# Projections summed kind by kind, and the substitution's transfers issued from POOL, in a hybrid encoder step

## The chip, the cores and the metric

One Trainium2 chip, one of its NeuronCores. The metric is the device time of one execution in microseconds (us). Engines: PE (TensorE, the matmuls; PEld is its weight load), DVE (VectorE), ACT (ScalarE), POOL (GpSimd), SP (SyncE, which here only issues transfers). Each engine works through its own list of instructions in the order in which the program lists them, and stands still where an instruction waits for a semaphore.

## What is computed

One layer of a streaming encoder, for 1024 prompt tokens and 64 sample tokens of width 1024: a modulation from a conditioning vector, a norm, one input projection whose columns feed four mixers, an output projection, a gated residual, then a SwiGLU feed-forward part. Cut to what matters:

```python
h = modulate(rms_norm(x), mod[0:3]);  u = h @ w_in
y = concat(conformer_conv(u), gated_deltanet(u), multi_scale_pool(u), stick_breaking_attention(u))
x = x + gate1 * (y @ w_out)
h = modulate(rms_norm(x), mod[3:6])
x = x + gate2 * ((silu(h @ w_gate) * (h @ w_up)) @ w_down)

# inside gated_deltanet, per chunk of 64 tokens and head:
lmat = where(strict, (kb @ k.T) * decay, 0)
sol  = triangular_solve(lmat + eye(64), rhs, lower=True, unit_diagonal=True)
S    = S * g_last + k_upd.T @ (u - w @ S)          # a scan over the chunks
```

## The kernel before

**Tokens and tiles.** The tokens run in two halves: A with 512 prompt tokens, B with the other 512 and the 64 sample tokens (576, in two PSUM chunks of 288 columns). Activations lie feature by feature: 8 tiles of 128 features by the tokens of a half. A weight tile is 128x1024: the 8 contraction tiles of 128 output features. The feed-forward part has 22 tiles of 128 hidden features (gate and up), taken in pairs, and a pair goes through `down` with a contraction of 2 tiles.

**Precision.** Every projection is done in split fp32: the weight as whi (rounded) and wlo (rest), the activation as hi and lo, and the product as wh·xh + wh·xl + wl·xh, three matmuls for each contraction tile, all summed in one PSUM bank. `load_w` (L313 to L324) loads a raw weight tile (SP), rounds it to whi (ACT, L117) and subtracts to wlo (DVE, L123); there are two buffers of each. The tiles hi0 to hi7 and lo0 to lo7 of the normed activations have one buffer each. They are written tile by tile by the modulation (ACT, L114, and DVE, L126).

**gemm_fm** (L342) is the projection: for each chunk of columns it takes a bank, and runs over the contraction tiles with all three products for each. It is called for the input projection (`gemm_out`, `sb_qk`), the output projection (`out_proj`), and gate, up and down of the feed-forward part (`ffn`). In the first stages it has two PSUM banks; late in the program (`wide`) it takes the eight banks of `BANKS` in turn, the bank "o" of the attention's output among them.

**The delta-rule part.** `dn_group` works on a group of up to four chunks, four heads: g1 and g2 (half A), g3 and g4 (half B), g5 (the sample tokens). The inverse of the triangular 64x64 matrix starts with its 16x16 diagonal blocks, by forward substitution on POOL, since a row of a block must become a row in one partition. The steps, each waiting for the one before: DVE writes nl, the strict products (L754); SP stores it to DRAM (nld, L777, two issues); SP loads the diagonal blocks back as rows (fsn, L782, four issues of 16x16x16, 16 KB each in runs of 64 bytes); POOL copies (L785) and does 29 small operations (L786, L135); SP stores the result (xd, L793, four issues); SP loads X (L796, two issues); PE turns X (pw0, L798), and the two doubling levels of the inverse follow. The whole chain is called nl to pw0 below.

**The rest around it.** `sb_attn` is the stick-breaking attention; POOL issues its loads of k, q and v (L501 to L507, and L540 to L544 for the sample tokens). At its end for the sample tokens, `sb_finish` takes four slices from the bank psOs: ACT copies a slice to sbo, DVE subtracts, SP stores it to DRAM (mixB), and the next slice needs the same sbo, which has one buffer.

**What sets the order.** The program is written operation by operation; a scheduler, told of priorities, puts the instructions of all parts into one list per engine. A change of one part re-lays the lists of all engines. A transfer keeps the queue of the engine that issues it.

Of the kernel before, what the change touches and what calls it, by code (L numbers as in the profile page):

```python
# [59 lines left out]
def hybrid_encoder_kernel(ctx: ExitStack, tc: tile.TileContext, io):  # L60
    nc = tc.nc
# [75 lines left out]
    def mm(out, lhsT, rhs, start=True, stop=True):  # L137
        return nc.tensor.matmul(out, lhsT=lhsT, rhs=rhs, start=start, stop=stop)  # L138
# [198 lines left out]
    def gemm_bank(name="pg"):  # L337
        turn[0] += 1
        pool, tag = BANKS[turn[0] % 8] if wide[0] else BANKS[0]
        return pool.tile([P, 512], F32, tag=tag, name=name)  # L340

    def gemm_fm(h, src, xh, xl, order, w=None, o=0):  # L342
        nk = len(order)
        wh, wl = w or load_w(src, nk * 128)
        out = []
        for c0, n in h.chunks:
            ps = gemm_bank()
            for i, k in enumerate(order):
                a, b = wh[:, o + k * 128:o + (k + 1) * 128], wl[:, o + k * 128:o + (k + 1) * 128]
                mm(ps[:, 0:n], a, xh[k][:, c0:c0 + n], i == 0, False)  # L350
                mm(ps[:, 0:n], a, xl[k][:, c0:c0 + n], False, False)
                mm(ps[:, 0:n], b, xh[k][:, c0:c0 + n], False, i == nk - 1)
            out.append((ps, c0, n))
        return out

    KALL = list(range(KT))
# [332 lines left out]
    def dn_group(h, feats, gate, D, ch0, nch, tok0, mtok0, S):  # L689
        w = 2 * nch * 64  # L690
# [3 lines left out]
        def T4(tag, bufs=1):  # L694
            return dn.tile([P, 576], F32, tag=tag, name=tag)[:, 0:128 * NCH]
# [13 lines left out]
        def PS(name):  # L709
            return PD(name)  # L710
# [31 lines left out]
        for pair in range(2):  # L742
            o = pair * nch * 64
# [24 lines left out]
        X, Y, W = T4("X"), T4("Y"), T4("W")  # L768
# [5 lines left out]
        nx = 2 * nch  # L774
        ext, ins = nld[samp_g], xd[samp_g]
        for hp in range(2):
            nc.sync.dma_start(out=ext[:, :, hp].rearrange("b i x c j -> (b i) (x c j)"), in_=nl[64 * hp:64 * hp + 64, 0:w])  # L777
        N = dn.tile([64, 256], F32, tag="fsn", name="fsn")[0:8 * nx]
        T = dn.tile([64, 256], F32, tag="fst", name="fst")[0:8 * nx]
        tmp = dn.tile([64, 64], F32, tag="fsu", name="fsu")[0:8 * nx]  # L780
        for q in range(4):
            nc.sync.dma_start(out=N[2 * nx * q:2 * nx * (q + 1)].rearrange("p (i j) -> p i j", j=16),  # L782
                              in_=ext[q, :, :, :, q].rearrange("i h x j -> (h x) i j"))
        N3, T3 = N.rearrange("p (i j) -> p i j", j=16), T.rearrange("p (i j) -> p i j", j=16)
        nc.gpsimd.tensor_copy(out=T, in_=N)  # L785
# [1 line left out]
        for k in range(1, 15):  # L787
            n = 15 - k
# [1 line left out]
            ptt(u3, N3[:, k + 1:16, k:k + 1].to_broadcast([8 * nx, n, k]), T3[:, k:k + 1, 0:k].to_broadcast([8 * nx, n, k]), ALU.mult)  # L790
            ptt(T3[:, k + 1:16, 0:k], T3[:, k + 1:16, 0:k], u3, ALU.add)
        for q in range(4):
            nc.sync.dma_start(out=ins[q, :, :, :, q].rearrange("i h x j -> (h x) i j"),  # L793
                              in_=T[2 * nx * q:2 * nx * (q + 1)].rearrange("p (i j) -> p i j", j=16))
        for hp in range(2):
            nc.sync.dma_start(out=X[64 * hp:64 * hp + 64, 0:w], in_=ins[:, :, hp].rearrange("b i x c j -> (b i) (x c j)"))  # L796
        pw = PS("pw0")
        flip(pw, blk(X))  # L798
        copy_a(Y[:, 0:w], pw[:, 0:w])
# [21 lines left out]
        for c in range(nch):  # L821
            pv2 = PS("pvn")
            for pair in range(2):
                j = (pair * nch + c) * 64
# [9 lines left out]
            for pair in range(2):  # L834
                j = (pair * nch + c) * 64
# [15 lines left out]
        m = T4("kbe").rearrange("p (a c) -> p a c", a=2)  # L851
# [183 lines left out]
    def out_proj(h):  # L1035
        hi, lo = [None] * KT, [None] * KT
        order = [6, 7, 4, 5, 0, 1, 2, 3]
        with tc.high_priority():
            spare = mix_tiles() if h.samp else None
            for i, k in enumerate(order):  # L1040
                if h.samp:
                    t = dn.tile([P, 576], F32, tag=f"f{1 + i % 2}", name="mixt")
                    hi[k], lo[k] = spare[2 * i], spare[2 * i + 1]
                else:
                    t = ST("mixt")
                    hi[k] = act.tile([P, 576], F32R, tag=f"hi{k}", name=f"hi{k}")
                    lo[k] = act.tile([P, 576], F32R, tag=f"lo{k}", name=f"lo{k}")
                nc.sync.dma_start(out=t[:, 0:h.n], in_=mixd[h.name][k])
                split(h, t, hi[k], lo[k])
            load_x(h, h.samp)  # L1050
        acc = new_acc()
        for m in range(KT):
            for ps, c0, n in gemm_fm(h, io["wout"][m], hi, lo, order):
                with tc.high_priority():
                    residual(h, m, 16, ps, c0, n)
            with tc.high_priority():
                sumsq(h, acc, m)
        with tc.high_priority():
            modulate(h, acc, s2, 24)

    def ffn(h):
# [4 lines left out]
        def gate(t):  # L1066
            silu = h.samp or t >= SILU_T
            a = ST("fa")
            for ps, c0, n in gemm_fm(h, io["wgate"][t], h.hi, h.lo, KALL):
                with tc.high_priority():  # L1070
                    if not silu:
                        copy_a(a[:, c0:c0 + n], ps[:, 0:n])
                    else:
                        act_(a[:, c0:c0 + n], ps[:, 0:n], ACTF.Silu)
            if not silu:
                with tc.high_priority():
                    e = ST("fe")
                    sigmoid_chain(e[:, 0:n_], a[:, 0:n_])
                    tt(a[:, 0:n_], a[:, 0:n_], e[:, 0:n_], ALU.mult)
            return a  # L1080
# [26 lines left out]
        a = gate(0)  # L1107
        for c in range(FT // FCH):
            g = []
            wide[0] = h.samp or c >= WIDE  # L1110
            for j in range(FCH):
# [4 lines left out]
                t = c * FCH + j + 1  # L1116
                a = gate(t) if t < FT else None
# [242 lines left out]
```

## Time and profile before

| | |
|---|---|
| median of 3 runs | 1493.4 us (1491.0, 1493.4, 1493.49) |
| the profiled execution | 1490.24 us, its span 1488.4 us |
| PE busy | 1404.4 us, 94% of the span, 9824 matmuls |
| DVE, ACT, POOL busy | 1027.0, 662.8, 88.4 us |
| mean granted TensorE clock | 0.97 of full speed |

The profile is of one execution; its own time stands beside the span, and the 1.84 us between them lie outside the span. Times in the rows are microseconds from the start of the span. Idle time of PE is named by what released it. The granted clock has two levels, 1.2 and 2.4 GHz; a stretch with a clock of 0.80 was for a part at the lower one.

### The profile page before, as it was taken

Reading aid. Unit: us, or ns where it says so; the run is one execution under the profiler, and the core shown is the slowest. Engines: PE = TensorE matmul, PEld = TensorE weight load, DVE = VectorE, ACT = ScalarE, POOL = GpSimd, SP = SyncE. Lnnn points to the kernel's source line nnn. Section 1 sums busy time; section 2 is a strip of 40 time slices with the busy share of each in tenths; the row PEclk is TensorE's granted clock in tenths of the full one; section 3 lists DMA queues with packets and bytes.
Section 4 is the critical chain, followed back from the end, with each engine's and each line's share of the span. In section 5 each row is a group of like instructions: output and inputs, shape, how many; then the busy total and the mean of one; then the engine's idle time right before and its main releaser. Section 6 shows DMA issues by size and latency. Waiting matters only on the chain.

```text
span 1488.4 us, 24781 instructions
## 1 busy us (share of the span) xinstructions
PE 1404.4 (94%) x9824; PEld 1223.0 (82%) x9824; DVE 1027.0 (69%) x1816; ACT 662.8 (45%) x1191; POOL 88.4 (6%) x196
## 2 busy tenths in 40 slices
PE   7999899978988799799999899999899999999999
PEld 5777788867966577587778688889799999999998
DVE  8788798855699999956766677664744555544444
ACT  4467554744474468656765432222522222222221
POOL 0003000300003000400111000000000000000000
PEclk8999999988999799999999999999999999999999
DMA  8685555555753422532324566542322222222222
GB/s 313 237 231 145 193 167 164 164 159 182 239 192 101 142 75 74 157 109 84 112 74 114 167 221 213 196 164 78 109 97 86 86 78 78 86 86 85 86 81 97
DMA packets 106867, 205.42 MB, mean 138 GB/s; under 512 B 39360, under 2 KB 49024, under 8 KB 106752
## 3 DMA queue, kind: packets, MB, share of 16 engines
q1 hardware_dynamic: 99936, 193.36, 39.6%
q0 software_dynamic: 6816, 10.49, 3.0%
q8 instruction: 77, 1.26, 0.3%
q14 instruction: 38, 0.31, 0.1%
HBM read 175.57 MB, written 28.24 MB: 137 GB/s over the span
## 4 chain that ended last, share of the span: by engine, by line
PE 66%; DVE 13%; DMA 10%; issue 3%; POOL 3%; ACT 3%; SPq 1%; DVEq 0%; ACTq 0%; POOLq 0%
PE pg L138 57%; DMA wadt<-in_wadat_dram 3%; DVE cy L126 3%; DVE wlo L123 2%; PE psC L141 1%; POOL fsu L135 1%; POOL fst L135 1%; PE pv L138 1%; PE psO L141 1%; PE z L141 1%; DVE lo L126 1%; DMA mixB<-sbo 1%; PE pw L138 1%; DVE junk L212 1%; ACT whi L117 1%
## 5 line engine op out<-in xcount | busy, mean ns | idle before, releaser
L138 PE MATMUL pg<-hi,whi 128*128 128x288 f32 (+1 forms) x1504 | 503.6, 336 | 12.6 <-ACT hi L114 4.4
L138 PE MATMUL pg<-hi,wlo 128*128 128x288 f32 (+1 forms) x1504 | 498.5, 332 | 4.8 <-DVE wlo L123 4.7
L138 PE MATMUL pg<-lo,whi 128*128 128x288 f32 (+1 forms) x1504 | 497.4, 331 | 1.6 <-DVE lo L126 1.6
L117 ACT ACTIVATE whi<-wraw 128x1024 fp32r<-128x1024 f32 (+2 forms) x192 | 199.7, 1041 | 479.2 <-PE pg L138 411.5
L138 PEld LDWEIGHTS pg<-hi,whi 128*128 128x128 f32 x1504 | 285.2, 190 | 41.9 <-ACT hi L114 5.0
L138 PEld LDWEIGHTS pg<-hi,wlo 128*128 128x128 f32 x1504 | 285.1, 190 | 30.4 <-DVE wlo L123 6.9
L138 PEld LDWEIGHTS pg<-lo,whi 128*128 128x128 f32 x1504 | 285.5, 190 | 26.7 <-issue 3.3
L123 DVE TENSOR_TENSOR wlo<-wraw,whi 128x1024 fp32r<-128x1024 f32 (+2 forms) x192 | 230.6, 1201 | 107.7 <-ACT whi L117 103.9
L138 PE MATMUL pg<-g,whi 128*128 128x288 f32 (+1 forms) x1056 | 252.2, 330 | 1.5 <-DVE xA L126 1.0
L138 PEld LDWEIGHTS pg<-g,whi 128*128 128x128 f32 x1056 | 177.7, 188 | 18.0 <-DVE xA L126 2.3
L138 PE MATMUL pg<-g,wlo 128*128 128x288 f32 (+1 forms) x528 | 171.9, 328 | 0.0
L126 DVE SCALAR_TENSOR_TENSOR xs<-pg,mod,xs 128x288 f32<-128x288 f32 (+2 forms) x288 | 106.6, 413 | 85.7 <-PE pg L138 82.5
L123 DVE TENSOR_TENSOR fa<-fa,pg 128x288 f32<-128x288 f32 (+1 forms) x66 | 35.1, 531 | 105.5 <-PE pg L138 101.8
L138 PEld LDWEIGHTS pg<-g,wlo 128*128 128x128 f32 x528 | 99.4, 188 | 7.5
L126 DVE SCALAR_TENSOR_TENSOR cy<-cvb,vec,cy 128x512 f32<-128x512 f32 (+1 forms) x120 | 93.7, 796 | 0.3
L126 DVE SCALAR_TENSOR_TENSOR xA<-pg,mod,xA 128x512 f32<-128x512 f32 x96 | 69.6, 746 | 18.7 <-PE pg L138 18.2
L212 DVE CUSTOM_DVE_ANT_0 wadt<-wadt,cb,vec 128x1024 f32<-128x1024 f32 x32 | 41.0, 1284 | 30.2 <-DMA wadt<-in_wadat_dram 30.2
L114 ACT ACTIVATE e<-e 128x512 f32<-128x512 f32 (+4 forms) x100 | 51.9, 519 | 0.7
L138 PE MATMUL pg<-mixs,whi 128*128 128x288 f32 x256 | 50.9, 295 | 0.0
L114 ACT ACTIVATE zs<-zs 128x512 f32<-128x512 f32 (+4 forms) x50 | 25.8, 517 | 47.3 <-DVE zs L123 47.2
L212 DVE CUSTOM_DVE_ANT_0 wads<-wads,cb,vec 128x1024 f32<-128x1024 f32 x32 | 41.0, 1280 | 4.8 <-DMA wads<-in_wadat_dram 4.6
L117 ACT ACTIVATE sh<-e 128x512 fp32r<-128x512 f32 (+4 forms) x50 | 25.8, 516 | 34.4 <-PE psC L141 22.7
(296 smaller groups left out, 1838.6 us busy)
## 6 DMA issues: line engine op xcount, KB each, us to landing
wraw<-in_wgate_dram SPq DMA_DIRECT2D x44, 512.0 KB, 3.3
wraw<-in_wup_dram SPq DMA_DIRECT2D x44, 512.0 KB, 3.3
wraw<-in_wdown_dram SPq DMA_DIRECT2D x44, 512.0 KB, 3.3
wadt<-in_wadat_dram SPq DMA_DIRECT2D x32, 512.0 KB, 5.1
wads<-in_wadat_dram SPq DMA_DIRECT2D x32, 512.0 KB, 4.3
wraw<-in_wfm_dram SPq DMA_DIRECT2D x30, 512.0 KB, 4.0
wraw<-in_wout_dram SPq DMA_DIRECT2D x16, 512.0 KB, 3.8
xA<-in_xa_dram SPq DMA_DIRECT2D x16, 256.0 KB, 5.8
```

The costliest lines, as they stand in the source:

```text
L114: nc.scalar.activation(out, in_, func, bias=bias, scale=scale)
L117: nc.scalar.activation(out, in_, ACTF.Copy)
L123: nc.vector.tensor_tensor(out=out, in0=a, in1=b, op=op)
L126: nc.vector.scalar_tensor_tensor(out, a, s, b, op0, op1)
L135: nc.gpsimd.tensor_tensor(out=out, in0=a, in1=b, op=op)
L138: return nc.tensor.matmul(out, lhsT=lhsT, rhs=rhs, start=start, stop=stop)
L141: nc.tensor.matmul(out, lhsT=lhsT, rhs=rhs, start=start, stop=stop, skip_group_check=True)
L212: nc.vector.tensor_tensor_reduce(out=junk, in0=w, in1=cbt[g], scale=1.0, scalar=V("b_ada", col), op0=ALU.mult, op1=ALU.add, accum_out=mod[ ...
```

## The change

Two things. First, in `gemm_fm` a projection now takes wh·xh for all contraction tiles, then wh·xl for all, then wl·xh for all, unless it is called with `streamed` set, which keeps the three products per tile; that is the first tile of the output projection and the first of the gate, in each half. The numbers and shapes of the matmuls are the same. Second, in `dn_group` the loads fsn, the stores xd and the loads X go from SP's queue to POOL's (10 issues per group, 50 in all); the store nld stays on SP. Lines behind gemm_fm move by 7.

```diff
-    def gemm_fm(h, src, xh, xl, order, w=None, o=0):
+    def gemm_fm(h, src, xh, xl, order, w=None, o=0, streamed=False):
...
-            for i, k in enumerate(order):
-                a, b = wh[:, o + k * 128:o + (k + 1) * 128], wl[:, o + k * 128:o + (k + 1) * 128]
-                mm(ps[:, 0:n], a, xh[k][:, c0:c0 + n], i == 0, False)
-                mm(ps[:, 0:n], a, xl[k][:, c0:c0 + n], False, False)
-                mm(ps[:, 0:n], b, xh[k][:, c0:c0 + n], False, i == nk - 1)
+            def prod(w, x, k, first, last):
+                mm(ps[:, 0:n], w[:, o + k * 128:o + (k + 1) * 128], x[k][:, c0:c0 + n], first, last)
+
+            if streamed:
+                for i, k in enumerate(order):
+                    prod(wh, xh, k, i == 0, False)
+                    prod(wh, xl, k, False, False)
+                    prod(wl, xh, k, False, i == nk - 1)
+            else:
+                for w, x in ((wh, xh), (wh, xl), (wl, xh)):
+                    for i, k in enumerate(order):
+                        prod(w, x, k, i == 0 and w is wh and x is xh, i == nk - 1 and w is wl)
...
-            nc.sync.dma_start(out=N[2 * nx * q:2 * nx * (q + 1)].rearrange("p (i j) -> p i j", j=16),
+            nc.gpsimd.dma_start(out=N[2 * nx * q:2 * nx * (q + 1)].rearrange("p (i j) -> p i j", j=16),
...
-            nc.sync.dma_start(out=ins[q, :, :, :, q].rearrange("i h x j -> (h x) i j"),
+            nc.gpsimd.dma_start(out=ins[q, :, :, :, q].rearrange("i h x j -> (h x) i j"),
...
-            nc.sync.dma_start(out=X[64 * hp:64 * hp + 64, 0:w], in_=ins[:, :, hp].rearrange("b i x c j -> (b i) (x c j)"))
+            nc.gpsimd.dma_start(out=X[64 * hp:64 * hp + 64, 0:w], in_=ins[:, :, hp].rearrange("b i x c j -> (b i) (x c j)"))
...
-            for ps, c0, n in gemm_fm(h, io["wout"][m], hi, lo, order):
+            for ps, c0, n in gemm_fm(h, io["wout"][m], hi, lo, order, streamed=m == 0):
...
-            for ps, c0, n in gemm_fm(h, io["wgate"][t], h.hi, h.lo, KALL):
+            for ps, c0, n in gemm_fm(h, io["wgate"][t], h.hi, h.lo, KALL, streamed=t == 0):
```

Three places show what the new lists look like.

**PE, the end of the sample tokens' attention** (psOs is its output bank, the last of BANKS; pg tiles are projections, here gates and ups of half A's feed-forward part). Before, at the last product of psOs, and then at the next tile in psOs' bank, pg_8631:

```order
L141 MATMUL psOs_6510<-ph_6577,v2s_6493 128x64
L141 MATMUL psOs_6510<-pl_6579,v2s_6493 128x64
L138 MATMUL pg_8667<-hi0_7149,wlo_8664 128x512
L138 MATMUL pg_8667<-hi1_7155,whi_8663 128x512
L138 MATMUL pg_8667<-lo1_7156,whi_8663 128x512
L138 MATMUL pg_8667<-hi1_7155,wlo_8664 128x512
```

```order
L138 MATMUL pg_8715<-hi7_7191,wlo_8712 128x512
L138 MATMUL pg_8631<-hi0_7149,whi_8627 128x512
L138 MATMUL pg_8631<-lo0_7150,whi_8627 128x512
L138 MATMUL pg_8631<-hi0_7149,wlo_8628 128x512
L138 MATMUL pg_8631<-hi1_7155,whi_8627 128x512
```

After:

```order
L141 MATMUL psOs_6510<-ph_6577,v2s_6493 128x64
L141 MATMUL psOs_6510<-pl_6579,v2s_6493 128x64
L138 MATMUL pg_8631<-hi0_7149,whi_8627 128x512
L138 MATMUL pg_8631<-hi1_7155,whi_8627 128x512
L138 MATMUL pg_8631<-hi2_7161,whi_8627 128x512
L138 MATMUL pg_8631<-hi3_7167,whi_8627 128x512
L138 MATMUL pg_8631<-hi4_7173,whi_8627 128x512
L138 MATMUL pg_8631<-hi5_7179,whi_8627 128x512
L138 MATMUL pg_8631<-hi6_7185,whi_8627 128x512
L138 MATMUL pg_8631<-hi7_7191,whi_8627 128x512
L138 MATMUL pg_8631<-lo0_7150,whi_8627 128x512
```

The kinds now follow one another within a tile, and pg_8631, which needs psOs' bank to be read out, has moved from 46 matmuls of 512 columns behind the last product of psOs to right behind it.

**DVE, ahead of nl of g3** (xA is the residual after the output projection of half A, acc the sum of squares of the norm behind it, cy the convolution, zs, sl and e the attention). Before:

```order
L123 TENSOR_TENSOR sl<-e,sh 128x512
L126 SCALAR_TENSOR_TENSOR gate<-gate,vec,ge 128x512
L126 SCALAR_TENSOR_TENSOR xA_6849<-pg,mod,xA_6849 128x512
L126 SCALAR_TENSOR_TENSOR xA_6851<-pg,mod,xA_6851 128x512
L126 SCALAR_TENSOR_TENSOR cy_6671<-cvb,vec,cy_6671 128x606
L123 TENSOR_TENSOR wlo<-wraw,whi 128x1024
L126 SCALAR_TENSOR_TENSOR nl<-pkk,W 128x512
```

After:

```order
L126 SCALAR_TENSOR_TENSOR xA_6859<-pg,mod,xA_6859 128x512
L123 TENSOR_TENSOR wlo<-wraw,whi 128x1024
L123 TENSOR_TENSOR at<-pkq,X 128x512
L130 TENSOR_SCALAR dnf_4852<-raw,vec 128x256
L123 TENSOR_TENSOR acc<-acc,sq 128x512
L130 TENSOR_SCALAR dnf_4852<-raw,vec 128x256
L123 TENSOR_TENSOR zs<-zs,psC 128x512
L126 SCALAR_TENSOR_TENSOR e<-zs,e 128x512
L126 SCALAR_TENSOR_TENSOR cy_6671<-cvb,vec,cy_6671 128x606
L126 SCALAR_TENSOR_TENSOR cy_6622<-cvb,vec,cy_6622 128x606
L126 SCALAR_TENSOR_TENSOR nl<-pkk,W 128x512
```

nl of g3 has moved behind later work of the output projection and behind a step of the attention that needs psC from PE.

**POOL, the start of g4's substitution.** Before:

```order
L503 DMA v_5815<-svA 128x512
L503 DMA v_5815<-svB 128x512
L785 COPY fst<-fsn 64x256
L501 DMA k_6039<-skA 128x512
L501 DMA k_6039<-skB 128x512
L507 DMA q_6041<-sqB 64x2x512
L786 TENSOR_SCALAR fst<-fst 64x16
```

After:

```order
L510 DMA v_5815<-svA 128x512
L510 DMA v_5815<-svB 128x512
L508 DMA k_6039<-skA 128x512
L508 DMA k_6039<-skB 128x512
L514 DMA q_6041<-sqB 64x2x512 x2
L789 DMA fsn<-nld_122 16x16x16 x4
L792 COPY fst<-fsn 64x256
L793 TENSOR_SCALAR fst<-fst 64x16
```

POOL now issues the loads fsn itself, behind the attention's loads k and q, which stood between its small operations before.

How much PE work the lists leave between nl and pw0 can be counted: from the last matmul that nl, by its place in DVE's list, has to come after, up to pw0's first. For g1, g3, g4 and g5 these are mostly matmuls of 512 columns, for g2 of 288; from 12 to 48 products of 64x64 and up to some 15 others lie there too.

| group | g1 | g2 | g3 | g4 | g5 |
|---|---|---|---|---|---|
| before: matmuls of 512 (g2: 288) columns | 122 | 106 | 104 | 104 | 94 |
| after | 145 | 130 | 62 | 129 | 148 |

## Rows read from the trace of the kernel before

**Rows 1.** Windows: us, PE, PEld, DVE, ACT, POOL busy (instructions), granted clock, DMA share, GB/s

```profile
300.00:350.00 50.00, 38.14 (x375) 31.33 (x375) 28.34 (x53) 21.20 (x45) 1.37 (x3) 0.80 0.55 160
...
450.00:525.00 75.00, 57.60 (x433) 42.75 (x432) 70.00 (x108) 34.91 (x59) 15.23 (x31) 0.84 0.41 120
...
600.00:650.00 50.00, 40.30 (x323) 30.83 (x322) 39.01 (x75) 25.36 (x55) 17.07 (x36) 0.90 0.45 129
...
825.00:850.00 25.00, 19.39 (x74) 13.54 (x73) 17.65 (x31) 6.89 (x13) 0.00 (x0) 0.86 0.50 159
850.00:875.00 25.00, 25.00 (x111) 20.44 (x110) 18.52 (x27) 13.15 (x17) 0.00 (x0) 1.00 0.77 261
...
1077.80:1480.00 402.20, 402.20 (x3034) 402.20 (x3035) 200.26 (x379) 93.30 (x126) 0.00 (x0) 1.00 0.25 83
```

**Rows 2.** Waits of PE over the span: total us, times, longest

```profile
PE pw L138 <- DMA X<-xd: 23.9, 4, 9.4
...
PE pg L138 <- DVE wlo L123: 4.7, 6, 2.0
PE pg L138 <- ACT hi L114: 4.4, 2, 3.5
```

**Rows 3.** Timeline of PE, pw0 of g2, g3, g4: start, us, idle before

```profile
306.08 0.44 PE L138 MATMUL pw<-cst,X 64*64 64x64 f32 x2 [9.41 <-DMA X<-xd]
471.30 0.45 PE L138 MATMUL pw<-cst,X 64*64 64x64 f32 x2 [5.51 <-DMA X<-xd]
631.44 0.44 PE L138 MATMUL pw<-cst,X 64*64 64x64 f32 x2 [7.82 <-DMA X<-xd]
```

**Rows 4.** Timeline of SP's queue, g2: start, us of issue

```profile
278.10 1.10 SPq L777 DMA_DIRECT2D nld<-nl  x2
281.02 2.15 SPq L782 DMA_DIRECT2D fsn<-nld  x4
...
300.23 1.79 SPq L793 DMA_DIRECT2D xd<-fst  x4
303.43 1.11 SPq L796 DMA_DIRECT2D X<-xd  x2
```

**Rows 5.** Timeline of POOL, g2: the copy ahead of the 29 small operations

```profile
285.53 0.39 POOL L785 COPY fst<-fsn 64x256 f32<-64x256 f32 x1 [14.05 <-DMA udnB<-ust]
```

**Rows 6.** Timeline of SP's queue, g4, where its chain begins

```profile
596.89 1.19 SPq L777 DMA_DIRECT2D nld<-nl  x2
...
601.86 0.43 SPq L782 DMA_DIRECT2D fsn<-nld  x1
```

**Rows 7.** DMA issues of the page's list: size, median us from issue to landing

```profile
k<-skA POOLq DMA_DIRECT2D x8, 256.0 KB, 4.9
...
X<-xd SPq DMA_DIRECT2D x8, 128.0 KB, 2.8
...
q2s<-sqB POOLq DMA_DIRECT2D x4, 128.0 KB, 3.3
...
fsn<-nld SPq DMA_DIRECT2D x16, 16.0 KB, 2.8
xd<-fst SPq DMA_DIRECT2D x16, 16.0 KB, 1.7
```

**Rows 8.** POOL's loads q over the span: ns to issue one, landings

```profile
L507 POOL DMA_DIRECT2D q<-sqA x8: 527/535/548, 132.2 to 270.9; - x8
...
DMA to landing us min/median/max: 3.4/4.4/9.2
```

**Rows 9.** Timeline of ACT at the end of the sample tokens' attention

```profile
837.81 0.22 ACT L117 ACTIVATE sbo<-psOs 64x64 f32<-64x64 f32 x1 [1.82 <-PE psOs L141]
843.33 0.22 ACT L117 ACTIVATE sbo<-psOs 64x64 f32<-64x64 f32 x1 [5.30 <-DMA mixB<-sbo]
845.60 0.22 ACT L117 ACTIVATE sbo<-psOs 64x64 f32<-64x64 f32 x1 [2.06 <-DMA mixB<-sbo]
...
849.14 0.22 ACT L117 ACTIVATE sbo<-psOs 64x64 f32<-64x64 f32 x1
```

**Rows 10.** Costliest groups of the page: DVE's subtraction for wlo, busy us, mean ns

```profile
L123 DVE TENSOR_TENSOR wlo<-wraw,whi 128x1024 fp32r<-128x1024 f32 (+2 forms) x192 | 230.6, 1201 | 107.7 <-ACT whi L117 103.9
```

## The prediction, made before any run of the changed kernel

> **What bounds the kernel now.** I read the windows first. From 1077.8 us to 1480 us PE is busy all the time at a clock of 1.00, 3034 matmuls in 402.20 us, so 0.133 us for one of 288 columns; from 850 to 875 it does 111 of 512 columns in 25.00 us, so 0.225 us each [rows 1]. There only fewer or smaller matmuls could help, and the change has neither. What can move is PE's idle time and the time at the lower clock, in four windows ahead of 850 us: idle are 11.9 us of 300 to 350, 17.4 of 450 to 525, 9.7 of 600 to 650 and 5.6 of 825 to 850 (each is the window less PE's busy time), and the clock there was 0.80, 0.84, 0.90 and 0.86 [rows 1]; with levels of 1.00 and 0.50 that is 20, 24, 10 and 7 us at 1.2 GHz. Next the waits of PE: the largest is pw0, which stood 23.9 us, in 4 of 5 groups, for the transfer X; wlo cost 4.7 us in 6 pieces, hi 4.4 us in two [rows 2]. The timeline of PE shows the pieces of pw0: 9.41 us at g2, 5.51 at g3, 7.82 at g4 [rows 3], so 23.9 less these, 1.2, at g1, and none at g5.
>
> Then the chain behind such a stall, at g2: nld issued at 278.10, fsn at 281.02, POOL's copy at 285.53, the stores xd at 300.23, X at 303.43 [rows 4, 5], pw0 at 306.08 [rows 3]: 28.0 us from nld, of which POOL's own arithmetic, from its copy to xd, has 14.7. PE has work for some 20 us meanwhile and stands for the rest. At g4 the chain takes from 596.89 [rows 6] to 631.44 [rows 3], 34.6 us.
>
> **The transfers on POOL.** SP and POOL take about the same time to issue: fsn 2.15 us for four, 0.54 each [rows 4], POOL's loads q 0.53 to 0.55 each [rows 8]. The landing differs: SP's fsn, xd and X have medians of 2.8, 1.7 and 2.8 us, POOL's loads 3.3 us at 128 KB (q2s) and 4.9 at 256 KB (k) [rows 7], and single loads q from 3.4 to 9.2 us [rows 8]. No row shows the substitution's small transfers on POOL, so the price has two ends. If all land as q2s does: +0.5, +1.6 and +0.5, less the 1.1 us by which SP's xd of 16 KB lands ahead of its X of 128 KB, so +1.5 us for the chain's three steps. If all land as k does: +2.1, +3.2 and +2.1, so +7.4 us. I take +4: the sizes, 16 KB and 128 KB, are nearer to q2s, but the runs of 64 bytes are short, and medians of POOL's loads lie between the two. A gain in the chain is not excluded, but only at g4, where SP split fsn around other work and issued the last of it 5.0 us after nld [rows 6], against 4.5 at g2 (281.02 plus three issues of 0.54, less 278.10). POOL's queue has more to give there: k and q stood between its operations, and now stand ahead of fsn. Of the 6.6 us by which g4's chain is the longer I take 4 as given back (ends 0 and 6.6).
>
> The Trainium skill, "DMA: Bandwidth & Descriptors", section "Issuing engine by pattern", speaks against this part: transfers issued from SP or ACT are generally the faster ones, and its "Specifications" put the first byte at about 0.6 us there and about 1 us from GpSimd. By that alone three steps would cost an estimated 1.2 us, less than the rows' lower end; the rows disagree with the size, not with the sign.
>
> What SP is relieved of is free: PE's waits for whi and wlo show no late weight transfer behind these issues that is worth over 2.0 us [rows 2].
>
> **The cover of the chain** is the PE work that the new lists leave between nl and pw0, as counted in the table ahead.
> - g1: 23 more matmuls, 23 x 0.225 = +5.2 us of cover. The chain is 4 us longer, and its fsn now stands behind POOL's loads q, which ended shortly before the copy; I take the stall from 1.2 to 2.7: **+1.5**.
> - g2: 24 x 0.133 = +3.2 us of cover against +4: **+1** (ends -2 and +4).
> - g3: 42 fewer, 42 x 0.225 = 9.5 us less cover, because nl moved behind the output projection of half A. With +4 the stall grows from 5.5 to 19, so +13.5. But the same window holds 17.4 - 5.5 = 11.9 us of other idle time, waits of the norm behind that output projection and of this group's levels. In the new DVE list the norm's sum of squares stands ahead of nl, so the norm runs while PE waits for X: I take 11 of the 11.9 as gone, and two of three dips of the clock merged (24 us at half speed become 16, which gives back 4): **-1.5** (ends -6 and +9).
> - g4: 25 x 0.225 = +5.6 of cover, 4 given back in POOL's queue, +4 for landings: the stall goes from 7.8 to 2.2, and about half of the dip behind it, worth 2.5 at most (half of the 5 us at 1.2 GHz that were not idle), with it: **-7** (ends -10 and -1).
> - g5: had no stall, and gains 54 x 0.225 = 12 us of cover: **0**, and with the cover gone at most the surcharge.
>
> Together -6.
>
> **The order of kinds.** wlo is asked for after 16 of 24 matmuls instead of after 2, some 3 us later at 0.225 us each; of the 4.7 us of waits for it I take **-3.5**. Against that, all eight hi are needed within the first 8 matmuls, 1.8 us instead of 5, and hi and lo, which have one buffer each, come free only in the last third of the last projection that reads them, so a norm behind it starts later. The nearest row is the wait for hi, 4.4 us in two, 3.5 the longest [rows 2]. The two `streamed` calls cover the output projection and the gate, not the first input projection of each half. I take **+2** (ends 0 and +7).
>
> **Behind the attention of the sample tokens.** The four slices of psOs left ACT at 837.81, 843.33, 845.60 and 849.14 [rows 9]: one buffer sbo, each slice behind the transfer of the one before, a trip of 2.3 to 5.5 us, the last also behind other work of ACT. Before, 46 matmuls, 10.4 us, stood on PE between psOs and the tile that needs its bank. Now there are none, and PE stands for the whole row of trips: three trips of 2.3 are 6.9, the old total 11.3. I take 9.6 against the 5.6 us that were idle in this window: **+4** (ends +1 and +8, the dip stays).
>
> **Sum:** -6 - 3.5 + 2 + 4 = -3.5. Against the profiled execution's 1490.24 us (1488.4 of span) that is 1486.7. The median of the runs is 3.2 above it, so the forecast is 1493.4 - 3.5, about **1490 us**.
>
> **The rivals.**
> 1. Slower: POOL's transfers land as its loads k do. The chain then gets +7.4 instead of +4; the 3.4 more stand on PE at g1, g2, g3 and g4: +13.6, so +10, 1503 us. For it: two of POOL's three streams have medians over 4 us [rows 7, 8]. Against it: those are 2 to 16 times larger. It decides when the surcharge passes 5.6 us (4 x 1.6 = 6.5 turns -3.5 into +3).
> 2. Slower still: POOL's descriptors wait for DVE. In 450 to 525 DVE was busy 70.0 of 75 us [rows 1], with instructions such as the one for wlo of 1.2 us [rows 10]. Were each of the ten issues to wait for the rest of one, 0.6 us on average, the chain would gain 6 us beyond the surcharge; on PE at g3, and at g4 beyond 1 us of slack, that is +11, so +8, 1501 us, and with the full 1.2 us up to 1513. Against it: POOL's issues of q never took over 0.55 us [rows 8]. The Trainium skill, "SBUF — State Buffer", section "SBUF: two separate sides", states the rule: while DVE runs in a mode with two ports, GpSimd cannot write its descriptors. The spread of q's landings, 3.4 to 9.2 us, allows it and does not show it.
> 3. Clearly faster: surcharge +1.5. Then g1 to g4 give 2.5 each, 10 in all, and the psOs term falls to its lower end: -3.5 - 10 - 3 = -16, 1477 us.
> 4. No change: g3's other waits come back behind pw0 instead of passing under it (3.5 of the 11): 1493 to 1494. The order shows that the change does what it says in both parts, so a change without effect is no case of its own.
>
> **How the numbers follow.** Forecast 0.38, rival 1 0.20, rival 2 0.08, rival 3 0.17, rival 4 0.17. A measurement of this kernel tells 0.2%, 3 us, from no change. Faster by over that: rival 3 and 0.27 of the forecast, 0.44; within: 0.11 of the forecast and most of rival 4, 0.22; slower: rivals 1 and 2 and the upper side of g3 and psOs, 0.34. The range takes in rival 3 with a little of g4's lower end, and rival 1 with 3 us of g3's upper end: 1474 to 1506. The forecast's own range is 1485 to 1495.
>
> **What would show it.** In the new profile: pw0 waiting for X about 2.7, 10, 19, 2 and 0 us; xd and X on POOL's queue landing in 3 to 4 us; the trips of sbo under a PE wait of 7 to 10 us; few waits for wlo; 1077.8 to 1480 as before. Wrong, if the landings pass 5 us, if g3's stall leaves the norm's waits behind it, or if PE stands at g4 still.

## The result, and the profile after

The changed kernel is slower: 1500.35 us (median of 14 runs, 1497.31 to 1506.36) against 1492.24 us for the kernel before (14 runs), a ratio of 1.006 with an interval of 1.0047 to 1.0074, some 8 us. The forecast was 1490 us. One execution of e2 below (4668 us) and one of e8 (2227.5 us, the one profiled) were far slower than the others of their kernel and are left out of the ratios and of every reading, and without them the two medians are 0.2 us lower. The profiled execution of the changed kernel took 1503.22 us, with a span of 1501.4; the one before had 1488.4.

The windows of the profile after (us, then PE, PEld, DVE, ACT, POOL busy, the granted clock, DMA share, GB/s), to be set beside [rows 1]:

```profile
300.00:350.00 50.00, 36.64 (x328) 28.78 (x326) 31.43 (x58) 27.95 (x60) 14.46 (x24) 0.80 0.53 152
...
450.00:525.00 75.00, 50.21 (x429) 36.72 (x429) 73.72 (x122) 34.64 (x58) 23.19 (x44) 0.80 0.39 117
...
600.00:650.00 50.00, 45.60 (x298) 34.82 (x295) 46.71 (x92) 33.03 (x69) 17.48 (x33) 0.97 0.38 108
...
825.00:875.00 50.00, 32.67 (x162) 25.67 (x160) 30.41 (x52) 19.82 (x38) 0.00 (x0) 0.83 0.55 177
```

PE's idle time is the window less its busy time: 13.4 us in 300 to 350 (11.9 before), 24.8 in 450 to 525 (17.4), 4.4 in 600 to 650 (9.7), and 17.3 in 825 to 875, where 5.6 were idle before, all of them in the first half [rows 1]. Of these four, two lost the most, 450 to 525 and 825 to 875, and one gained. Behind 1100 us nothing changed: PE's idle time there was 0.3 us up to 1485 us before, and 0.3 us up to 1490 us after.

The waits of PE after (total us, times, longest), to be set beside [rows 2]:

```profile
PE pg L138 <- DVE sbo L123: 15.2, 1, 15.2
PE pw L138 <- DMA X<-xd: 9.7, 2, 8.6
PE psC L141 <- DVE sl L123: 8.8, 1, 8.8
PE pw L138 <- DVE plo L126: 6.5, 1, 6.5
...
PE pv L138 <- DVE lo L126: 3.8, 2, 3.1
```

The largest wait is new, 15.2 us in one piece, for sbo: the slices of psOs. The one for X has shrunk from 23.9 us to 9.7 (16.2 with the 6.5 put down to plo, which were X's too, below), and waits for wlo no longer stand in the list (4.7 before). A new piece of 8.8 us in the attention (psC for sl) lies in the window of g3. The pieces in the timeline of PE (start, us, and the idle time before with its releaser), those of [rows 3] and the new ones:

```profile
323.17 0.47 PE L138 MATMUL pw<-cst,X 64*64 64x64 f32 x2 [6.46 <-DVE plo L126]
```

and of the later stretches

```profile
488.59 0.80 PE L141 MATMUL psC<-sl,u_r 128*128 128x512 f32 x1 [8.79 <-DVE sl L123]
...
506.79 2.38 PE L138 MATMUL pw<-cst,X 64*64 64x64 f32 x32 [8.61 <-DMA X<-xd]
...
664.54 0.33 PE L138 MATMUL pw<-cst,X 64*64 64x64 f32 x2 [1.07 <-DMA X<-xd]
```

```profile
865.20 3.75 PE L138 MATMUL pg<-hi,whi 128*128 128x512 f32 x8 [15.16 <-DVE sbo L123]
```

At g2 the wait of 6.46 us is put down to plo, at g3 8.61 to X; g4 stood 1.07 us and g1 and g5 not at all. The first is X too: it was issued at 320.44 (below), and in the run e1, with the same list, the same wait is put down to X:

```profile
320.43 0.47 PE L138 MATMUL pw<-cst,X 64*64 64x64 f32 x2 [6.01 <-DMA X<-xd]
```

The chain of g2 on POOL's queue, for [rows 4, 5]:

```profile
286.21 2.30 POOL L789 DMA_DIRECT2D fsn<-nld  x4 [38.11 <-DMA nld<-nl]
...
291.70 0.54 POOL L792 COPY fst<-fsn 64x256 f32<-64x256 f32 x1 [1.55 <-DMA fsn<-nld]
...
310.04 2.36 POOL L800 DMA_DIRECT2D xd<-fst  x4 [0.29 <-POOL fst L135]
320.44 1.06 POOL L803 DMA_DIRECT2D X<-xd  x2 [8.04 <-DVE e L126]
```

Here xd was issued by 312.40 and X could be issued only at 320.44, 8.0 us later. On SP that step took 1.4 us (300.23 and 1.79 of issue, to 303.43) [rows 4].

And the four slices of psOs on ACT, for [rows 9], and their additions on DVE (`sb_finish` adds there; it does not subtract, as the description ahead has it):

```profile
850.42 0.22 ACT L117 ACTIVATE sbo<-psOs 64x64 f32<-64x64 f32 x1
857.09 0.22 ACT L117 ACTIVATE sbo<-psOs 64x64 f32<-64x64 f32 x1 [6.45 <-DMA mixB<-sbo]
860.32 0.22 ACT L117 ACTIVATE sbo<-psOs 64x64 f32<-64x64 f32 x1 [3.01 <-DMA mixB<-sbo]
...
864.04 0.22 ACT L117 ACTIVATE sbo<-psOs 64x64 f32<-64x64 f32 x1
```

```profile
852.81 0.22 DVE L123 TENSOR_TENSOR sbo<-psOs,sbo 64x64 f32<-64x64 f32 x1
...
856.97 1.28 DVE L212 CUSTOM_DVE_ANT_0 wads<-wads,cb,vec 128x1024 f32<-128x1024 f32 x1 [2.60 <-DMA wads<-in_wadat_dram]
...
858.29 0.22 DVE L123 TENSOR_TENSOR sbo<-psOs,sbo 64x64 f32<-64x64 f32 x1
860.57 0.22 DVE L123 TENSOR_TENSOR sbo<-psOs,sbo 64x64 f32<-64x64 f32 x1 [2.06 <-ACT sbo L117]
...
864.84 0.22 DVE L123 TENSOR_TENSOR sbo<-psOs,sbo 64x64 f32<-64x64 f32 x1
```

The four slices left ACT within 13.6 us, 850.42 to 864.04, where it had been 11.3 before [rows 9]; and now PE stood under them from 850.04 to 865.20, with nothing of its own to do. The granted clock was near its lower level in that stretch (us, then as in [rows 1]):

```profile
850.00:865.20 15.20, 0.04 (x1) 0.03 (x1) 6.16 (x12) 1.96 (x6) 0.00 (x0) 0.57 0.45 147
865.20:875.00 9.80, 7.62 (x24) 5.78 (x24) 3.87 (x5) 3.33 (x5) 0.00 (x0) 0.80 0.45 139
```

### The profile page after: what moved, and what is told of

Read it like the earlier page. It is cut to its first block, busy times and chain, and to the rows that moved or that the text cites. A ratio compares the mean times of both kernels' runs of the same rounds, so it can differ in the third digit from the quotient of the medians.

```text
span 1501.4 us, 24776 instructions
## 1 busy us (share of the span) xinstructions
PE 1403.9 (94%) x9824; PEld 1226.2 (82%) x9824; DVE 1024.4 (68%) x1816; ACT 671.5 (45%) x1191; POOL 125.9 (8%) x246
## 4 chain that ended last, share of the span: by engine, by line
PE 73%; DVE 12%; DMA 7%; ACT 3%; issue 3%; POOL 1%; SPq 1%; DVEq 0%; POOLq 0%; ACTq 0%
PE pg L138 61%; PE psC L141 2%; DVE wlo L123 2%; DVE cy L126 2%; DMA wadt<-in_wadat_dram 2%; PE psO L141 1%; PE pv L138 1%; PE z L141 1%; DVE junk L212 1%; PE pw L138 1%; DVE dnf L126 1%; DVE xA L126 1%; DVE wadt L212 1%; DMA mixt<-mixB 1%; POOL fst L135 1%
## 5 line engine op out<-in xcount | busy, mean ns | idle before, releaser
L138 PE MATMUL pg<-hi,whi 128*128 128x288 f32 (+1 forms) x1504 | 303.8, 337 | 23.3 <-DVE sbo L123 15.2
L138 PE MATMUL pg<-lo,whi 128*128 128x288 f32 (+1 forms) x1504 | 296.8, 332 | 0.5 <-DVE lo L126 0.5
L138 PE MATMUL pg<-hi,wlo 128*128 128x288 f32 (+1 forms) x1504 | 294.8, 331 | 0.0
L138 PEld LDWEIGHTS pg<-hi,whi 128*128 128x128 f32 x1504 | 240.3, 191 | 54.4 <-issue 19.0
L138 PEld LDWEIGHTS pg<-lo,whi 128*128 128x128 f32 x1504 | 238.9, 190 | 25.5 <-issue 2.8
L138 PEld LDWEIGHTS pg<-hi,wlo 128*128 128x128 f32 x1504 | 236.7, 188 | 24.7 <-issue 3.5
L138 PE MATMUL pg<-g,whi 128*128 128x288 f32 (+1 forms) x1056 | 221.9, 331 | 4.6 <-ACT g L117 3.4
L138 PE MATMUL pg<-g,wlo 128*128 128x288 f32 (+1 forms) x528 | 130.6, 329 | 0.0
L114 ACT ACTIVATE fa<-pg 128x288 f32<-128x288 f32 (+1 forms) x52 | 23.0, 441 | 51.9 <-PE pg L138 51.8
L117 ACT ACTIVATE g<-fa 128x512 fp32r<-128x512 f32 (+1 forms) x44 | 28.9, 657 | 24.9 <-DVE fa L123 24.7
```

Source lines behind the costliest of these rows:

```text
L114: nc.scalar.activation(out, in_, func, bias=bias, scale=scale)
L117: nc.scalar.activation(out, in_, ACTF.Copy)
```

## The experiments

Theory A: the loss is PE's wait behind psOs, because the tile that needs its bank comes right behind it. Theory B: the transfers on POOL cost. Theory C: the kinds taken apart cost, by hi and lo that come free later. All times are medians, with their ratio to the kernel before in the same set of runs (1491.4 to 1494.5 us) and its interval of 95%. There were four sets, e1 to e4, e5 to e8, e9 to e12 and e13 to e15. Since the kernel before differs by up to 3 us between them, runs of different sets are compared by their ratios; an uncertainty that stands with such a difference is an estimate worked from the two or three intervals.

**e1, the changed kernel with the four slices in one go.**

```diff
-        for hd in range(4):
-            sb_finish(HB, hd, psO, hd * 64, 64, 512)
+        o = SS("sbo")
+        copy_a(o[64:128, 0:256], psO[64:128, 0:256])
+        tt(o[0:64, 0:256], psO[0:64, 0:256], o[64:128, 0:256], ALU.add)
+        for hd in range(4):
+            r0 = 64 * (hd % 2)
+            nc.sync.dma_start(out=mixd["B"][6 + hd // 2, r0:r0 + 64, 512:576], in_=o[0:64, hd * 64:hd * 64 + 64])
```

> The changed kernel, with the four slices of psOs taken in one go: one copy on ACT, one addition on DVE, then the four stores; all engines' lists ahead of that place are the same. Theory A (PE stands 15.2 us behind the attention of the sample tokens, because the tile that needs psOs' bank comes right behind it): three round trips of sbo go, the wait falls to 2 to 6 us, and the time falls by 9 to 13 us, to 1488 to 1491 us, about that of the kernel before. Theory B (the transfers issued from POOL are what costs): the trips are no longer on PE, but the loss lies ahead of them, so the time stays within 3 us of 1500. Theory C (taking the kinds apart costs, through hi and lo that come free later): as B.

Measured: 1486.75 us, 0.995 (0.9932 to 0.9968). The wait is 3.48 us in the timeline of PE:

```profile
850.75 3.78 PE L138 MATMUL pg<-hi,whi 128*128 128x512 f32 x8 [3.48 <-DVE sbo L123]
```

13.6 us came back by the medians (16 by the ratios), more than the 9 to 13 that theory A had asked for, and B and C fall as the account of the whole loss. With this one place cured the change is faster than the kernel before.

**e2, the kernel before with the same edit.**

> The kernel before with the same edit of the four slices. Theory A: there 46 matmuls covered the trips, so little is to be had: 0 to 4 us faster, 1488 to 1492 us. If the edit itself saves time whatever stands behind psOs (a rival to A's reading of e1), it gains here as much as in e1.

Measured: 1493.09 us, 0.9994 (0.9978 to 1.001): nothing. The edit is worth its 13.6 us only where the bank's next tile stands right behind.

**e3, the kinds alone** (the change with fsn, xd and X issued from SP).

> The kinds apart as in the change, all of the substitution's transfers on SP as before. Its lists leave 18.5, 20.7 and 20.9 us of cover at g2, g3 and g4, and 10.8 us (48 matmuls) behind psOs. Theory A: the wait behind psOs is gone; X stalls of about 10 us at each of g2, g3, g4 stay (chain 28 to 31 us): 1490 to 1497 us. Theory B: as fast as before or faster, 1487 to 1493. Theory C: as slow as the change, 1498 to 1502.

Measured: 1505.07 us, 1.0078 (1.0052 to 1.0104): slower, as theory C alone had it, and by somewhat more than its 1498 to 1502. But its mechanism isn't there. PE's longest new wait, at the norm of half B's input, and what ACT did then:

```profile
172.88 0.59 PE L138 MATMUL pv<-whi,hi 128*128 128x264 f32 x1 [9.97 <-ACT hi L114]
```

```profile
169.28 0.63 ACT L114 ACTIVATE cve<-cvg 128x512 f32<-128x512 f32 x1 [9.79 <-DMA cvg<-ucvA]
...
172.12 4.35 ACT L114 ACTIVATE hi<-xB,mod 128x512 fp32r<-128x512 f32 x10
```

ACT stood 9.8 us for a load of the convolution (cvg) that its list had put ahead of hi; the buffers of hi were not what it waited for. So a theory D: the input projections' new lists cost.

**e4, the transfers on POOL alone** (the kernel before with fsn, xd and X issued from POOL).

> The substitution's transfers on POOL as in the change, the three products per contraction tile as before. Its lists leave 37.6, 27.1, 32.4 and 27.2 us of cover at g1 to g4, and 8.1 us behind psOs. Theory A: X stalls of 0 to 2, 5 to 7, 2 to 4 and 5 to 7 us, the wait behind psOs 3 to 7 us: 1484 to 1492 us. Theory B: slower, 1496 to 1502 us, with X landing late. Theory C: as before, 1490 to 1493.

Measured: 1486.36 us, 0.9963 (0.9945 to 0.9981): faster, and theory B falls, though POOL's chain is longer: from nld to the last issue of X it took 32.9, 29.1, 35.5 and 36.5 us at g1 to g4, against 30.5, 26.4, 29.0 and 32.7 before, 3.8 us more on average. By the counts in the expectation the lists laid with POOL's queue in them leave more cover.

**e5, the changed kernel with psOs' bank out of the turn.**

```diff
-    BANKS = [(ps_mm, "mm"), (ps_mm, "mm"), (ps_dn, "dn"), (ps_dn, "dn"), (ps_cv, "cv"), (ps_sb, "z"), (ps_sb, "c"), (ps_sb, "o")]
+    BANKS = [(ps_mm, "mm"), (ps_mm, "mm"), (ps_dn, "dn"), (ps_dn, "dn"), (ps_cv, "cv"), (ps_sb, "z"), (ps_sb, "c")]
...
-        pool, tag = BANKS[turn[0] % 8] if wide[0] else BANKS[0]
+        pool, tag = BANKS[turn[0] % 7] if wide[0] else BANKS[0]
```

> The changed kernel with its four slices as they were, but psOs' bank is taken out of the projections' turn (7 banks in place of 8). PE's list is the same up to psOs; the first matmul that the slices hold up now comes 25.6 us of PE work later. Theory A (that bank, with nothing between, is what PE stands for): the wait of 15.2 us goes, 1486 to 1490 us, as in the run where the slices were taken in one go (1486.75). Rival (the slices' own work on ACT, DVE and SP delays what the projections need, whatever the bank): 1495 to 1501 us.

Measured: 1477.18 us, 0.9905 (0.9884 to 0.9926), 23.2 us below the changed kernel and below what was expected. The slices take as long as ever:

```profile
846.91 0.22 ACT L117 ACTIVATE sbo<-psOs 64x64 f32<-64x64 f32 x1 [1.14 <-PE psOs L141]
...
852.07 0.22 ACT L117 ACTIVATE sbo<-psOs 64x64 f32<-64x64 f32 x1 [3.27 <-DMA mixB<-sbo]
...
857.37 0.22 ACT L117 ACTIVATE sbo<-psOs 64x64 f32<-64x64 f32 x1 [2.08 <-DMA mixB<-sbo]
...
863.94 0.22 ACT L117 ACTIVATE sbo<-psOs 64x64 f32<-64x64 f32 x1 [2.07 <-DMA mixB<-sbo]
```

17.0 us from the first to the last, and PE runs through it at full clock:

```profile
450.00:525.00 75.00, 49.81 (x396) 36.10 (x395) 72.17 (x119) 33.71 (x56) 24.08 (x44) 0.77 0.36 101
...
825.00:875.00 50.00, 50.00 (x244) 40.09 (x243) 40.47 (x65) 21.39 (x36) 0.00 (x0) 1.00 0.68 228
```

Not the trips cost, but what stood behind them. The window of g3 is as bad as in the changed kernel (25.2 us idle).

**e9, the kernel before with the same edit.**

> The kernel before, with psOs' bank out of the projections' turn, as in the run of the changed kernel that took 1477.2 us. The lists ahead of psOs are those of before; behind it 20.0 us of PE work cover the slices in place of 10.3. Theory A: the kernel before lost little there (5.6 us idle in its window): 1485 to 1491 us. Rival (seven banks in turn are worth some 14 us whatever stands behind psOs): 1475 to 1480 us.

Measured: 1488.98 us, 0.9971 (0.9955 to 0.9987), so 2.6 us. Of the 23.2 us of e5 the place behind psOs has thus some 20 us to itself in the changed kernel (by the ratios 19, give or take 4).

**e6 and e7, the kinds in part of the projections, transfers on SP.** In e6 the input projections keep three products per tile (`streamed=True` in gemm_out and sb_qk), in e7 gate, up and down do.

> The kinds apart in the output projection and the feed-forward part, three products per tile in the input projections, all transfers on SP. The run with all kinds apart and SP's transfers took 1505 us, with 10.0 us of PE's idle time at the norm of half B's input (pv waits for hi, ACT stands for the load cvg ahead of it in its list) and 26.6 us for X. Theory D (the input projections' new lists cost that): this falls to 1491 to 1497 us. Rival E (the kinds in the feed-forward part cost): stays at 1500 to 1506 us.

> The kinds apart in the input and output projections only, three products per tile in gate, up and down, all transfers on SP. Theory D: the loss stays, 1500 to 1506 us, with the wait of pv for hi near 170 us. Rival E: falls to 1491 to 1495 us.

Measured: e6 1491.35 us, 0.9997 (0.9981 to 1.0013), e7 1508.48 us, 1.0109 (1.0086 to 1.0132). The loss of e3 stays with the input projections' kinds and goes without them: theory D, E falls. e7 has its wait of pv for hi too, 7.9 us.

**e8 and e10, POOL's transfers with either cure of psOs** (e4 with the slices in one go; e4 with seven banks).

> Three products per tile, the substitution's transfers on POOL (1486.4 us), and the four slices of psOs in one go. The lists are the same up to psOs, where that run waited 3.0 us for sbo. Theory A: 1 to 4 us less, 1482 to 1486 us, the fastest so far.

> Three products per tile, the substitution's transfers on POOL, psOs' bank out of the turn. Transfers on POOL alone took 1486.4 us, and 1478.8 with the slices in one go. If what the slices cost there is the wait behind the bank: 1476 to 1482 us; if the one copy itself saved the time: 1484 to 1488.

Measured: 1478.82 us, 0.9921 (0.9894 to 0.9948), and 1480.32 us, 0.9919 (0.9901 to 0.9937). The two cures are worth the same, 6.3 and 6.6 us by the ratios, each give or take 4 to 5. That is twice the 3.0 us of e4's wait, but not clearly more than it.

**e11, as e10, with the stores xd back on SP.**

> As the run before it in this list, but the stores xd go back to SP. On POOL they land 1.9 to 8.2 us after the last issue, on SP 1.3 to 1.7. Theory F (POOL's queue is slow for xd): X is issued some 3 us sooner after xd, and with nearly the same cover at g2 and g4 (28.2 and 27.0 against 27.1 and 27.2 us) their stalls fall by 3 us each, g3's stays: 1472 to 1479 us, xd landing within 2 us. Rival (the landing hangs on what else the DMA engines carry at that moment): xd lands as late on SP, and the time is that of the run without this edit or more.

Measured: 1493.17 us, 1.0004 (0.9989 to 1.0019). The step is as theory F had it: at g2, xd to X on POOL in e10, and in e11 xd on SP and X on POOL,

```profile
293.44 2.27 POOL L793 DMA_DIRECT2D xd<-fst  x4 [0.29 <-POOL fst L135]
299.32 1.06 POOL L796 DMA_DIRECT2D X<-xd  x2 [3.60 <-DVE sl L123]
```

```profile
304.51 1.80 SPq L793 DMA_DIRECT2D xd<-fst  x4
```

```profile
308.14 1.10 POOL L796 DMA_DIRECT2D X<-xd  x2 [3.65 <-ACT sh L117]
```

3.6 us behind the last issue of xd in the one (299.32 less 295.71), 1.8 in the other (308.14 less 306.31). But pw0 then came 5.5 and 4.1 us behind the issue of X at g3 and g4, 1.6 and 1.7 in e10, and the time rose by 13 us: as a price for the kernel theory F falls. At g3 and g4 X itself landed later, 6.7 and 5.4 us from its issue against 2.8 and 2.5 in e10; from its last issue to pw0 the DMA engines were busy 1.01 and 0.84 of the time, against 0.71 and 0.52. At g3 of e11 SP, done with xd at 473.00, issued four loads of weights from 473.11 to 474.91, just ahead of X at 474.84 on POOL. Nor does e11 compare the two queues for xd under equal conditions: while SP issued xd there, the DMA engines were busy only 0.05 to 0.19.

**e12, the changed kernel with seven banks and the input projections per tile.**

> The changed kernel with psOs' bank out of the turn and the input projections back to three products per tile. Covers 37.6, 27.1, 32.4 and 29.8 us at g1 to g4, 19.1 behind psOs. Theory D (the kinds cost in the input projections, where the norms' hi and lo are late): 1468 to 1476 us, the fastest of all. If the input projections' kinds are harmless once the transfers are on POOL: 1477, as with all kinds apart.

Measured: 1469.76 us, 0.9848 (0.9829 to 0.9867): 30.6 us below the changed kernel, the fastest of all, and theory D holds with POOL's transfers too: the input's kinds cost 7.4 us (e5 against e12; by the ratios 8.5, give or take 4). Without them the kinds gain 10.6 us (e12 against e10, one set). Its windows:

```profile
300.00:350.00 50.00, 40.79 (x425) 33.70 (x423) 28.28 (x53) 23.38 (x50) 2.19 (x4) 0.83 0.51 164
...
450.00:525.00 75.00, 56.59 (x460) 42.46 (x458) 70.43 (x111) 35.75 (x65) 16.13 (x30) 0.82 0.45 113
...
600.00:650.00 50.00, 43.85 (x346) 33.74 (x345) 37.34 (x58) 27.16 (x55) 13.09 (x22) 0.97 0.44 131
...
825.00:875.00 50.00, 49.91 (x216) 40.16 (x215) 34.99 (x51) 21.75 (x31) 0.00 (x0) 1.00 0.66 215
```

**e13 to e15, what in the input's kinds costs.** e13 is e5 with the last tile of each half's input projection per tile; e14 is e12 with that tile alone by kinds; e15 is e12 with the gate per tile.

> The changed kernel with psOs' bank out of the turn (1477.2 us), and the last tile of each half's input projection (the second of pl) back to three products per tile. Theory G (the kinds in the input cost because hi and lo of a half, one buffer each, come free only in the last third of the last projection, so the norm behind waits): most of the 7.4 us to the run with all input projections per tile come back, 1469 to 1473 us. Rival H (the whole lists of the input stages differ, the cover of g3 above all: 16.3 us here, 32.4 with the input per tile): 1475 to 1479 us.

> The fastest run so far (1469.8 us: transfers on POOL, bank out, input projections per tile), with the last tile of each half's input projection by kinds. Theory G: loses most of the 7.4 us, 1474 to 1478. Rival H: only what its list moves, g4's cover of 21.0 in place of 29.8 us among it: an X stall of 6 to 9 us more at g4 and none at the norms.

> The fastest run so far with the gate's projections back to three products per tile as well. PE has no idle time where most of these run, so by the work alone nothing changes; the lists of all engines are laid again (covers 37.6, 27.1, 32.4, 27.3 and 24.5 behind psOs). If a new list alone moves the time by as much as single parts of the change did, this differs from 1469.8 us by 5 us or more; if not, 1467 to 1473 us.

Measured: 1475.56 us, 0.9874 (0.985 to 0.9897); 1478.23, 0.9912 (0.9878 to 0.9946); 1475.56, 0.9868 (0.9844 to 0.9893). In this set the kernel before took 1494.48 us, 2.9 more than in e12's and 3.1 more than in e5's, so the medians can't be set beside 1477.2 and 1469.8 as they stand. By the ratios e13 is 4.6 us faster than e5, give or take 4.7, and decides nothing between G and H by its time. e14 is 9.6 us slower than e12, give or take 6, as G had it in size, but not at a norm: PE stood for X of g2, which rival H had looked for at g4,

```profile
317.52 2.33 PE L138 MATMUL pw<-cst,X 64*64 64x64 f32 x32 [14.58 <-DMA X<-xd]
```

```profile
303.89 2.27 POOL L800 DMA_DIRECT2D xd<-fst  x4 [0.30 <-POOL fst L135]
314.79 1.05 POOL L803 DMA_DIRECT2D X<-xd  x2 [8.63 <-DMA xd<-fst]
```

since X's issue on POOL waited 8.6 us for xd to land; in e12 pw0 of g2 stood 5.95 us. e15, which only puts the gate's products in another order, is 3.0 us slower than e12 by the ratios, give or take 4.6 (its runs from 1468.1 to 1476.7 take in those of e12): a move by a new list alone isn't shown by it.

What the input's kinds cost lies in the lists that come of them, and no run shows hi and lo late because their buffers came free late. The row that goes with the loss is the wait of the attention for sl, in the window of g3, here in e5 and e13:

```profile
482.22 0.80 PE L141 MATMUL psC<-sl,u_r 128*128 128x512 f32 x1 [8.64 <-DVE sl L123]
477.62 0.79 PE L141 MATMUL psC<-sl,u_r 128*128 128x512 f32 x1 [9.95 <-DVE sl L123]
```

With all input projections by kinds the longest such wait is 8.6 to 8.8 us (the changed kernel, e1, e5) and 4.6 to 4.8 with the transfers on SP (e3, e7), in e13 it is still 9.95, and in e6, e12, e14 and e15 it is 0.8, 0.6, 1.2 and 1.9. In the changed kernel DVE worked without a gap from 475.66 to 487.86 at convolution, modulation, norms and wlo, which stood ahead of sl in its list. No run moved sl alone, so that this wait is the whole loss is not shown.

## Why the prediction was wrong

**The step that failed is the one on the attention's end.** "I take 9.6 against the 5.6 us that were idle in this window: +4 (ends +1 and +8, the dip stays)." The mechanism and the place were right; the term was three to five times too small. The wait was 15.2 us and not 9.6. The three trips were 6.7, 3.2 and 3.7 us, 13.6 in all (850.42 to 864.04), more than the old total of 11.3 that the working took as its upper end; and 1.5 us at both ends (850.04 to 850.42, and 864.04 to 865.20) were left out of it. In the first trip the addition stood behind a step of the modulation on DVE (852.81, 2.4 us after its copy), in the second trip behind another such step, for whose load DVE had stood 2.60 us, and the last addition stood behind the tile mixs (864.84). And the dip did not stay: the clock of 825 to 875 fell from 0.93 (7 us at 1.2 GHz, worked from 0.86 in 825 to 850 and 1.00 behind it [rows 1]) to 0.83 (17 us). But 13 of these 17 us lie in the wait itself, where PE had nothing to lose; behind it, from 865.20 to 875, some 4 us were at 1.2 GHz, and 3 more from 875 to 885 (0.83), which costs at most 3.7 us. Measured, the term is +13.6 by the medians and +15.5 by the ratios (e1 against e2), +20.6 and +18.8 (e5 against e9), each give or take 4, and not +4. It alone turns the forecast round: with the other terms as predicted, -7.5 and 13.6 to 20.6 make +6 to +13, and the measured change is +8. That 1500 us still lies between 1474 and 1506 is luck: the upper part of the range stood there for late landings on POOL.

**The rest of the sum came out about right as a sum, in part by luck, since not piece by piece.** With psOs' bank out in both, the change is 1477.18 against 1488.98 us, -11.8 (by the ratios -9.8, give or take 4); the terms said -7.5. POOL's transfers are -8.7 there (e10 against e9; predicted -6 with their cover), the kinds -3.1 (e5 against e10, by the ratios -2.1, give or take 4; predicted -3.5 and +2).
- g4: as said. The wait fell from 7.82 to 1.07 us (predicted 2.2), idle time of its window by 5.3 us, and its clock rose from 0.90 to 0.97.
- g1 and g2: 0 and 6.5 us, where 2.7 and 10 were predicted; at g2 PE had lost 3.4 and 3.5 us just ahead, in the attention and in the norm of q and k, and so stood less for X.
- g3: wrong, "-1.5". The wait for X was 8.61 us and not 19, and the idle time of the window still rose by 7.4 us, at a clock of 0.80 instead of 0.84. PE stood first in the attention, 8.79 us for sl, and only then for X: the norm's waits did not pass under one long stall, other waits were added to it.
- The surcharge of POOL: +4 predicted, +3.8 in e4 and +6.0 in the changed kernel (nld to the last issue of X 35.6, 40.1, 33.5 and 33.7 us, against 30.5, 26.4, 29.0 and 32.7). Not all steps share it alike, as the price "as k lands" had them: of the 24.3 us more over g1 to g4 the step from xd to X has 14.5, and the most of that at g1, g2 and g4 (below).
- "What SP is relieved of is free": this looked only at PE's waits for weights. Relieved of xd and X, SP issues its own transfers beside them (at g2 six from 307.68 to 312.68), and the long landings of xd fall beside such transfers (below); how much of the surcharge that is, no run shows.
- wlo: the 4.7 us are gone, as said. hi and lo, +2: the waits of PE for hi and lo are as before in sum, but the input's kinds cost 7.4 us (e5 against e12; 8.5 by the ratios) by their lists. G, the mechanism behind the +2, isn't seen in any row; the wait for sl, 8.8 us, was in no term.

**The rivals.** The first, slower by POOL's landings, came out with the right sign for the wrong reason: e4 has them and is faster. The second, POOL held by DVE, isn't what g2 shows: while xd took 8 us to land, DVE was busy 2.6 of 10 us,

```profile
310.00:315.00 5.00, 0.89 (x2) 0.72 0.36 38
315.00:320.00 5.00, 1.72 (x3) 0.96 0.94 338
```

and none of its instructions there took over 1.3 us; at g3, where DVE was busy all the time, xd landed in 1.9 us (below). Its argument that POOL's issues of q never took over 0.55 us held for the loads from sqA alone; those from sqB took 0.60 to 0.68. The Trainium skill, "SBUF — State Buffer", section "SBUF: two separate sides", has the rule that GpSimd can't write its descriptors while DVE runs in a mode with two ports; no run here shows it. The slow side that had no rival was the one that decided, since the psOs term stood in the sum with an end of +8.

## What to carry to other kernels

Where the order of all engines is laid anew, look in the new list for the next user of each single buffer or PSUM bank that is read out slowly, and price that wait from the stop to the last read, with what stands ahead of each step on each engine, not from the trips alone. Give such a bank no next user (seven banks in place of eight cost nothing here) before judging anything else: the change was 8 us slower with it and 10 to 12 faster without. Look in the new list, too, for steps that other engines wait for and that now stand behind a long row of other work, as sl did on DVE. And compare runs of different sets by their ratios, with the uncertainty of both: here a difference of two ratios is uncertain by 4 to 6 us, as much as single parts of this change are worth.

## What the runs showed of the hardware

The four stores xd, 16 KB each in runs of 64 bytes (4 KB at g5), let X be issued 1.3 to 1.7 us behind their last issue from SP (kernel before, five groups), and 4.8, 8.0, 1.9, 5.5 and 4.6 us from POOL (changed kernel, g1 to g5, of which some 1.1 at g4 and 3.3 at g5 are other issues in between). In e1 and e5 it was 6.7 to 7.0, 7.6 to 8.2, 1.9 and 5.5 to 5.7 us at g1 to g4. This is no comparison of the two queues alone, since the DMA engines were not equally busy. From the last issue of xd to X (us, DVE busy, granted clock, DMA share, GB/s), at g3, g1 and g2 of the changed kernel, and at g1 of e3, where xd was on SP:

```profile
502.11:504.02 1.91, 1.91 (x4) 0.50 0.19 17
159.89:164.73 4.84, 3.96 (x8) 1.00 0.96 324
312.40:320.44 8.04, 2.16 (x5) 0.92 0.62 220
```

```profile
155.81:159.39 3.58, 0.64 (x2) 1.00 0.49 138
```

Where the DMA engines were busy 0.10 to 0.25 of the stretch, POOL's step took 1.9 to 2.1 us (g3 of the changed kernel, e1, e5 and e13, g4 of e15, g5 of e12 and e13), with 2.5 and 2.7 at g5 of e14 and e4. The kernel before had 0.06 to 0.47 in these stretches; where SP's xd fell beside other transfers, it took 2.4 (e6, g4, 0.87), 2.7 (e7, g1, 0.65) and 3.6 us (e3, g1, 0.49, and 0.97 in the first 1.3 us). So POOL's long steps go with other transfers. They are longer than SP's few busy ones, and how much of that is the queue is open, since no run took the other transfers away. At g2, beside the 8.0 us, SP's load wraw also took 9.3 us to land, and wadt 9.9 (medians before 4.0 and 5.1). The lists suggest why SP had the quiet stretches: SP issues the loads of weights too, and at g2 of the kernel before it issued nothing between 292.63 and 300.23, where it stood for xd. That is argued from the lists and not tested.

The Trainium skill, "DMA: Bandwidth & Descriptors", section "Specifications", has about 0.6 and 1 us to the first byte on the two paths, so an estimated 0.4 us between them. The quiet steps, 1.9 to 2.1 against 1.3 to 1.7 us, agree with it in size; the long ones are many times that.

The loads fsn, as small, show no such difference (1.3 to 4.4 us from SP, 1.5 to 4.9 from POOL in the changed kernel), nor does X where PE stood for it (1.5 to 2.4 us from its last issue to pw0 from SP, 1.7 to 3.0 from POOL).
